# Hybrid four-branch layer on one core: the recurrent branch woven at weight 48 instead of 26, the last tiles' modulation split between two engines, and the next branch's operand loaded three chunks earlier in the merge

## The chip, the cores and the metric

The kernel runs on one core of a Trainium2 chip. The metric is device microseconds of one execution. The five engines run their own instruction queues in order: PE (TensorE, matrix products), ACT (ScalarE), DVE (VectorE), POOL (GpSimd) and SP (SyncE, which here only issues DMAs). ACT issues DMAs too.

## The reference

Two layers (DEPTH = 2) work on 1024 latent tokens and 256 context tokens of width 1024. One input projection feeds four mixers and their gates; the mixers' outputs are merged and projected:

```python
p_lat = (layer_norm(x) * (1.0 + scale) + shift) @ w_in
...
ya = merge_heads(neighbourhood_attention(q, k, v, kc, vc, na_rel_bias))     # branch A
yb = merge_heads(prefix_attention(q, k, v, kc, vc, MLA_SCALE))              # branch B
yc, yc_c = rglru_mixer(lat[6], cx[6], ...)                                  # branch C, recurrent
yd = merge_heads(prefix_attention(q, k, v, kc, vc, GQA_SCALE))              # branch D
...
acc = sum(jax.nn.sigmoid(ms[i]) * ((ys[i] * jax.nn.silu(zs[i])) @ w_branch[i]) for i in range(N_BRANCH))
x_new = layer_norm(DEEPNORM_ALPHA * x + gate * (acc @ w_out)) * ln_g + ln_b
```

The recurrent branch computes, for each direction, `r` and `i` by sigmoids of small products, `a = exp(log_a)`, `u = sqrt(1 - a*a) * i * x`, and a linear scan along the tokens.

## The kernel before

All ten 128-token tiles (two of context, eight latent) stay in SBUF as pairs `xh`, `xl`: a value in float32 is split into a rounded high part and a low rest, and a product is three matmuls (high by high, high by low, low by high: L299 to L301 and L307 to L309). The split is done by `hi_lo` (ACT copies the high part at L312, DVE subtracts at L313) or, for weights, by `split_w` (L263, L264).

A layer runs in these stages, and the names of tiles in the profile begin with the stage that made them.

- `g_proj`, the projection of branch D.
- A stage in which two generators are woven. The main one chains `m_proj` (branch B, 12 steps), one step that loads the first attention operands, and `a_proj` (branch A: ten 512-column tiles for q and k, then ten 256-column tiles for v; some 20 steps). The other is `lru_steps` (branch C), for each of two halves of 128 channels: a projection, a convolution, then for each direction the products with sigmoids (L515), tanh (L522), exp (L523), sqrt (L528), and the scans; then `put_u`, which multiplies the branch's output with its gate. That is 24 steps a half in layer 0 and 20 in layer 1. `weave` always advances the stream with the least `(steps done + 0.5) / weight`: the main one has weight `W_A = 30`, the other `W_B = 26`. A weight is only a rate; a stream that is left goes on alone.
- Attention for the three branches (`g_att`, `m_att`, `a_att`), with the products of half of the merge gates ("gates", `g_att__mm` and so on) as filler for PE. Before it, `cut_memory` gives the same SBUF out anew; a new tile waits until the old ones at its place have been read.
- `merge`: for each branch in the order 2, 3, 1, 0 and each of 8 chunks of 128 columns, the gate's product (even chunks) or its stored value from DRAM (odd chunks), its sigmoid, the branch product, and the sum. At the head of each branch `load_u` brings the branch's output in from DRAM and splits it. All of this goes through the rotating pool `tmp` of 3 buffers, and all loads through SP's queue. In layer 0 the next layers' modulation vectors (`mod`) are computed beside it.
- `outp`: output projection, residual, two norms. In layer 0 `xm_tile` then makes the next layer's `xh`, `xl` for a tile: for each half of 4 blocks, four PE transposes into a PSUM bank (`tbank`), four ACT operations that scale and shift (L243; a DVE form stands in L245 but `V_ACT = 4` never takes it), and a split. `tbank` has two banks, and a third one (the bank of attention's `pv`) while `wide_t[0]` is set, which it isn't in `outp`.

The engines' final order is made by a scheduler that keeps dependences and follows program order as a priority, so instructions of neighbouring steps mix.

Of the kernel before, what the change touches and what calls it, by code (L numbers as in the profile page):

```python
# [17 lines left out]
KC = D // 128  # L18
# [3 lines left out]
TT = NT // 128  # L22
# [7 lines left out]
V_ACT = 4  # L30
# [4 lines left out]
X_ACT = (0, 2)  # L35
M_ORDER = (2, 3, 1, 0)
W_A = 30
W_B = 26
Z_0, GATE_0 = 2, 10
UNITS = [(2, 3), (5, 3), (8, 2)]  # L40
AHEAD = 2
# [6 lines left out]
def hybrid_kernel(ctx: ExitStack, tc, a):  # L48
# [27 lines left out]
    def nm(s):  # L76
        ids[0] += 1
        return f"{phase[0]}__{s}_{ids[0]}"
# [4 lines left out]
    def weave(*streams):  # L83

        live = [[0, n, label, gen] for label, gen, n in streams]
        while live:
            s = min(live, key=lambda s: (s[0] + 0.5) / s[1])
            phase[0] = s[2]
            s[0] += 1
            if next(s[3], live) is live:  # L90
                live.remove(s)
# [11 lines left out]
    def chain(*parts):  # L103
        for label, gen in parts:
            while True:
                phase[0] = label
                if next(gen, parts) is parts:
                    break
                yield

    def mm():
        return ps_mm.tile([128, 512], F32, tag="mm", name=nm("mm"))

    turns = [0, 0, 0]
    wide_t = [False]

    def sbank():

        turns[1] = (turns[1] + 1) % 3
        return wide[:, 512 * turns[1]:512 * turns[1] + 512]  # L120

    def tbank():
        turns[2] = (turns[2] + 1) % 3
        if wide_t[0] and not turns[2]:
            return ps_v.tile([128, 512], F32, tag="pv", name=nm("t"))
        return ps_t.tile([128, 512], F32, tag="t", name=nm("t"))
# [13 lines left out]
    def kept(which, dt=F32, w=NT, s="kept"):  # L140

        return kv.tile([128, w], dt, tag=which, name=nm(s))

    def slot(dt=F32, w=NT, s="sl"):
        return cut["sl"].tile([128, w], dt, tag="sl", name=nm(s))

    def tmp(w=512, dt=F32):
        return tp.tile([128, w], dt, tag="tmp", name=nm("tmp"), bufs=3)
# [81 lines left out]
    def xm_tile(t, xn, mc, xh, xl):  # L230
        s = 1 if t < CT else 0
        ts = slice(t * 128, (t + 1) * 128)
        for h in range(2):
            pt = tbank()
            v = tmp()
            for i in range(4):
                k = 4 * h + i
                pe.transpose(pt[:, i * 128:(i + 1) * 128], xn[:, k * 128:(k + 1) * 128], ident)
            for i in range(4):
                k = 4 * h + i  # L240
                o, src = v[:, i * 128:(i + 1) * 128], pt[:, i * 128:(i + 1) * 128]
                if i < V_ACT:
                    act.activation(o, src, AF.Identity, bias=mc[:, s, k:k + 1], scale=mc[:, s, 8 + k:9 + k])  # L243
                else:
                    dve.tensor_scalar(o, src, mc[:, s, 8 + k:9 + k], mc[:, s, k:k + 1], ALU.mult, ALU.add)  # L245
            v3 = v.rearrange("p (k t) -> p k t", k=4)
            hi_lo(xh[:, 4 * h:4 * h + 4, ts], xl[:, 4 * h:4 * h + 4, ts], v3)
# [22 lines left out]
    def load_w(src, shape, far=False, by_pool=False):  # L270
        n = 1
        for d in shape[1:]:
            n *= d
        raw = cut["wp"].tile([128, 512], F32, tag="wraw", name=nm("wraw"), bufs=2)
        dst = raw[:, :n]
        if len(shape) == 3:
            dst = dst.rearrange("p (a b) -> p a b", a=shape[1])
        sp.dma_start(dst, src)
        return split_w(raw, shape, far, by_pool)
# [4 lines left out]
    def load_chunk(w3, by_pool=False):  # L284

        out = []
        nk = w3.shape[1]
        for k0 in range(0, nk, 4):
            kk = min(4, nk - k0)
            hi, lo = load_w(w3[:, k0:k0 + kk, :], [128, kk, 128], by_pool=by_pool)  # L290
            out += [(hi[:, i, :], lo[:, i, :]) for i in range(kk)]
        return out
# [10 lines left out]
    def mm_b(ps, ws, xs, first=True, last=True):  # L303
        nk = len(ws)
        for k in range(nk):
            (wh, wl), (xh, xl) = ws[k], xs(k)
            pe.matmul(ps, wh, xh, start=first and k == 0, stop=False)  # L307
            pe.matmul(ps, wh, xl, start=False, stop=False)  # L308
            pe.matmul(ps, wl, xh, start=False, stop=last and k == nk - 1)  # L309

    def hi_lo(hi, lo, src):
        act.copy(hi, src)  # L312
        dve.tensor_sub(lo, src, hi)  # L313

    def layer(l, xh, xl, need_ctx, gate, finish, side, ahead=None):
# [11 lines left out]
        def xs_g(g):  # L327
            gs = slice(g[0], g[0] + g[1])
            return lambda k: (xh[:, k, gs], xl[:, k, gs])
# [471 lines left out]
        def a_steps():  # L801
            wa = load_rows(w_in, C_A, 512)
            prev = None
            for t, ps in project(wa, lambda t: 0 if t >= q0t else 256, 512):
                c0 = 0 if t >= q0t else 256
                y = tmp()
                if c0 == 0:
                    act.activation(y[:, :256], ps[:, :256], AF.Copy, scale=0.125)
                act.copy(y[:, 256:], ps[:, 256:])  # L809
                if prev:  # L810
                    put_t(*prev)
                prev = qk_a, t, c0 // 128, [y[:, c:c + 128] for c in range(c0, 512, 128)]
                yield
            put_t(*prev)
            wv = load_rows(w_in, C_AV, 256)
            for t, ps in project(wv, lambda t: 0, 256):
                put_v(v_a, t, ps[:, :256].rearrange("p (h e) -> p h e", e=64))
                yield
# [126 lines left out]
        def first_loads():  # L945
            next(att)
            yield


        weave(("", chain((f"m_proj{l}", m_steps()), (f"g_att{l}", first_loads()), (f"a_proj{l}", a_steps())), W_A),  # L950
              (f"lru{l}", lru_steps(), W_B))
        wide_t[0] = False
# [10 lines left out]
        def load_u(i, keep):  # L963
            uh, ul = [], []
            for c in range(2):
                if keep and c == 0:
                    th, tl = kept("k", F32R, s="uh"), kept("v", F32R, s="ul")
                else:
                    th, tl = slot(F32R, s="uh"), slot(F32R, s="ul")
                for g in qgroups:  # L970
                    gs = slice(g[0], g[0] + g[1])
                    t = tmp(g[1])
                    sp.dma_start(t, u_d[i][c, :, gs])
                    hi_lo(th[:, gs], tl[:, gs], t)
                uh.append(th)
                ul.append(tl)
            return uh, ul

        def merge():
            for bi, i in enumerate(M_ORDER):  # L980
                uh, ul = load_u(i, bi % 2 == 0)
                for c in range(KC):
                    w = None if (i, c) in gate_d else load_chunk(a["w_chunks"][l, GATE_0 + i * KC + c])
                    wb = load_chunk(a["w_branch"][l, i, c])
                    if bi == 0:
                        acc[c] = slot(s="acc")
                    for g in qgroups:
                        gs = slice(g[0], g[0] + g[1])
                        sgm = tmp()
                        if w is None:  # L990
                            pm = sgm
                            sp.dma_start(sgm[:, :g[1]], gate_d[i, c][:, gs])
                        else:
                            pm = mm()
                            mm_b(pm[:, :g[1]], w, xs_g(g))
                        act.activation(sgm[:, :g[1]], pm[:, :g[1]], AF.Sigmoid)
                        pb = sbank()
                        mm_b(pb[:, :g[1]], wb, lambda k: (uh[k][:, gs], ul[k][:, gs]))
                        if bi == 0:
                            dve.tensor_mul(acc[c][:, gs], pb[:, :g[1]], sgm[:, :g[1]])  # L1000
                        else:
                            dve.tensor_mul(sgm[:, :g[1]], pb[:, :g[1]], sgm[:, :g[1]])  # L1002
                            (pool if w is None else dve).tensor_add(acc[c][:, gs], acc[c][:, gs], sgm[:, :g[1]])  # L1003
                        yield
# [29 lines left out]
        chunks = list(range(x0, NT, 256))  # L1034


        phase[0] = f"outp{l}"
        gain = [[cut["wp"].tile([128, 512], F32, tag=tag, name=nm(src)) for _ in range(2)]
                for tag, src in (("whi", "ln_g"), ("wlo", "ln_b"))]
# [126 lines left out]
    def fin0(t, Y, later):  # L1166
        if t >= CT:
            sp.dma_start(x1[(t - CT) * 128:(t - CT + 1) * 128, :], Y)
        layer_norm(Y, LN2_ACT)
        later.append(partial(xm_tile, t, Y, mc1["m"], xh, xl))  # L1170
# [96 lines left out]
```

## Time and profile before

| | |
|---|---|
| time, median of 3 runs | 2960.34 us (2957.03 to 2962.0) |
| time of the profiled execution | 2960.92 us |
| its span, first to last instruction | 2959.1 us |
| PE, DVE, ACT, POOL busy | 94%, 51%, 41%, 14% of the span |
| TensorE clock granted, mean | 0.977 of full speed |
| HBM traffic | 101 GB/s over the span |

The profile gives, for one execution, when each instruction ran on its engine, what ended each idle time, and the granted TensorE clock (1.0 is the upper of its two levels, 2.4 GHz; 0.5 the lower, 1.2 GHz). PE is the busiest engine, so idle PE and PE at the lower clock are what can be won.

### The profile page before, as it was taken

The page shows a single profiled execution, that of the slowest core. Times are in us where ns is not written, and L with a number is a line of the kernel's source. Part 1 is how long each engine was busy: PE and PEld are TensorE (multiplying, and loading weights), DVE is VectorE, ACT ScalarE, POOL GpSimd, SP SyncE. Part 2 cuts the span into 40 slices and gives each one's busy share as a digit, 9 for nine tenths or more (in the row PEclk, how much of TensorE's full clock was granted, in tenths as well). Part 3 has the DMA queues.
Part 4 walks back from the last instruction along what each step waited for, and adds up shares of the span by engine and source line. Part 5 has one row for each costly group of instructions (what it writes and reads, how often), then busy time and mean ns, then how long its engine had stood idle before and what let it go on. Part 6 is the DMA issues. An engine that isn't in the chain of part 4 may idle for free.

```text
span 2959.1 us, 40218 instructions
## 1 busy us (share of the span) xinstructions
PE 2790.4 (94%) x14458; PEld 2253.0 (76%) x14458; DVE 1508.0 (51%) x3069; ACT 1219.0 (41%) x2631; POOL 418.8 (14%) x507
## 2 busy tenths in 40 slices
PE   7997979999999999899999798999999999999998
PEld 3785858888888887677767576778888888777776
DVE  5644266555555552232458554356555556533456
ACT  4344256445455542222234434346545455522230
POOL 1210020110111100111222120012111111001131
PEclk9998989999999999999999898999999999999999
DMA  6333322222223333333332333423222323222232
GB/s 248 115 107 102 107 72 84 84 84 87 88 88 123 103 98 111 104 120 104 124 98 90 91 103 111 117 74 102 80 93 78 106 103 126 87 94 87 86 109 91
DMA packets 240424, 301.83 MB, mean 102 GB/s; under 512 B 27488, under 2 KB 160096, under 8 KB 240224
## 3 DMA queue, kind: packets, MB, share of 16 engines
q1 hardware_dynamic: 134368, 225.58, 24.2%
q10 hardware_dynamic: 105856, 73.68, 8.0%
q8 instruction: 114, 1.87, 0.3%
q14 instruction: 86, 0.70, 0.1%
HBM read 217.11 MB, written 82.07 MB: 101 GB/s over the span
## 4 chain that ended last, share of the span: by engine, by line
PE 75%; DVE 7%; DMA 4%; ACT 4%; issue 2%; POOL 2%; ACTq 1%; SPq 0%; DVEq 0%; POOLq 0%
PE wide L639 6%; PE merge__mm L307 4%; PE merge__mm L308 4%; PE merge__mm L309 4%; PE wide L307 3%; PE wide L308 3%; PE wide L309 3%; PE m_att__t L584 3%; PE g_att__t L584 2%; PE a_att__mm L307 2%; PE a_att__mm L308 2%; PE a_att__mm L309 2%; PE m_att__mm L309 2%; PE m_att__mm L308 2%; PE m_att__mm L307 2%
## 5 line engine op out<-in xcount | busy, mean ns | idle before, releaser
L307 PE MATMUL merge__mm<-xh,merge__whi 128*128 128x512 f32 (+1 forms) x640 | 243.0, 380 | 0.9 <-ACT a_att__tmp L934 0.9
L308 PE MATMUL merge__mm<-xl,merge__whi 128*128 128x512 f32 (+1 forms) x640 | 239.6, 374 | 0.0
L309 PE MATMUL merge__mm<-xh,merge__wlo 128*128 128x512 f32 (+1 forms) x640 | 239.4, 374 | 0.0
L313 DVE TENSOR_TENSOR m_att__pl<-m_att__t,m_att__ph 128x384 fp32r<-128x384 f32 (+1 forms) x248 | 122.1, 508 | 117.2 <-ACT m_att__ph L312 78.8
L263 ACT CAST merge__whi<-merge__wraw 128x256 fp32r<-128x256 f32 (+1 forms) x128 | 65.6, 513 | 255.6 <-PE merge__mm L308 176.7
L1002 DVE TENSOR_TENSOR merge__tmp<-wide,merge__tmp 128x512 f32<-128x512 f32 (+1 forms) x120 | 76.5, 637 | 184.8 <-PE wide L309 161.2
L1003 POOL TENSOR_TENSOR merge__acc<-merge__acc,merge__tmp 128x512 f32<-128x512 f32 (+1 forms) x60 | 79.2, 1320 | 585.9 <-DVE merge__tmp L1002 585.8
L307 PEld LDWEIGHTS merge__mm<-xh,merge__whi 128*128 128x128 f32 x640 | 120.6, 188 | 44.5 <-issue 19.9
L312 ACT CAST m_att__ph<-m_att__t 128x384 fp32r<-128x384 f32 (+1 forms) x248 | 105.0, 439 | 115.3 <-PE m_att__t L584 103.5
L313 DVE TENSOR_TENSOR g_att__pl<-g_att__t,g_att__ph 128x384 fp32r<-128x384 f32 (+1 forms) x228 | 111.3, 514 | 79.6 <-ACT g_att__ph L312 58.4
L307 PE MATMUL wide<-merge__uh,merge__whi 128*128 128x256 f32 (+1 forms) x320 | 127.4, 398 | 20.4 <-ACT merge__uh L312 11.5
L264 DVE TENSOR_TENSOR merge__wlo<-merge__wraw,merge__whi 128x256 fp32r<-128x256 f32 (+1 forms) x128 | 71.0, 555 | 141.2 <-ACT merge__whi L263 134.3
L309 PEld LDWEIGHTS merge__mm<-xh,merge__wlo 128*128 128x128 f32 x640 | 120.8, 189 | 23.9 <-issue 0.4
L308 PEld LDWEIGHTS merge__mm<-xl,merge__whi 128*128 128x128 f32 x640 | 120.8, 189 | 22.3
L312 ACT CAST g_att__ph<-g_att__t 128x384 fp32r<-128x384 f32 (+1 forms) x228 | 97.7, 446 | 69.3 <-PE g_att__t L584 65.3
L307 PE MATMUL a_att__mm<-xh,a_att__whi 128*128 128x512 f32 (+1 forms) x320 | 123.8, 387 | 0.0
L641 DVE TENSOR_SCALAR_CACHE_REDUCE m_att__p<-wide 128x1280 f32<-128x1280 f32 (+1 forms) x72 | 98.7, 1371 | 42.1 <-PE wide L639 41.8
L309 PE MATMUL a_att__mm<-xh,a_att__wlo 128*128 128x512 f32 (+1 forms) x320 | 120.1, 377 | 0.0
L639 PE MATMUL wide<-g_att__ks,g_att__q 128*128 128x512 f32 (+1 forms) x400 | 103.5, 365 | 17.5 <-DVE g_att__p L641 16.3
L308 PE MATMUL a_att__mm<-xl,a_att__whi 128*128 128x512 f32 (+1 forms) x320 | 120.0, 375 | 0.0
L299 PE MATMUL a_proj__mm<-a_proj__whi,xh 128*128 128x256 f32 (+1 forms) x320 | 112.0, 351 | 8.1 <-ACT a_proj__tmp L809 4.5
L308 PE MATMUL wide<-merge__ul,merge__whi 128*128 128x256 f32 (+1 forms) x320 | 119.6, 374 | 0.0
(418 smaller groups left out, 7919.4 us busy)
## 6 DMA issues: line engine op xcount, KB each, us to landing
merge__wraw<-in_w_chunks_dram SPq DMA_DIRECT2D x64, 256.0 KB, 2.9
mod__wm<-in_w_mod_dram SPq DMA_DIRECT2D x64, 256.0 KB, 3.0
g_proj__wm<-in_w_mod_dram SPq DMA_DIRECT2D x16, 512.0 KB, 9.8
a_att__wraw<-in_w_chunks_dram SPq DMA_DIRECT2D x32, 256.0 KB, 2.7
merge__wraw<-in_w_branch_dram SPq DMA_DIRECT2D x64, 128.0 KB, 2.1
merge__tmp<-start__gates SPq DMA_DIRECT2D x32, 256.0 KB, 3.2
merge__tmp<-outp__gates SPq DMA_DIRECT2D x32, 256.0 KB, 3.4
g_att__wraw<-in_w_chunks_dram SPq DMA_DIRECT2D x28, 256.0 KB, 2.7
```

The lines of the kernel that those rows point to most:

```text
L264: (pool if by_pool else dve).tensor_sub(lo[:, :n], raw[:, :n], hi[:, :n])
L299: pe.matmul(ps, xh, wh[:, n0:n1], start=first and k == 0, stop=False)
L307: pe.matmul(ps, wh, xh, start=first and k == 0, stop=False)
L308: pe.matmul(ps, wh, xl, start=False, stop=False)
L309: pe.matmul(ps, wl, xh, start=False, stop=last and k == nk - 1)
L312: act.copy(hi, src)
L313: dve.tensor_sub(lo, src, hi)
L584: pe.transpose(tb[:, i * 128:(i + 1) * 128], pts[q0 + i][:, col:col + 128], ident)
L639: pe.matmul(wide[:, c0:c0 + w], qs[:, j, qi * 128:(qi + 1) * 128], k[:, c0:c0 + w], start=j == 0, stop=j == len(ks) - 1)
L641: dve.tensor_scalar(pt[:, :nk], wide[:, :nk], -scale, None, ALU.mult, ALU.min, accum_out=nb)
L1002: dve.tensor_mul(sgm[:, :g[1]], pb[:, :g[1]], sgm[:, :g[1]])
L1003: (pool if w is None else dve).tensor_add(acc[c][:, gs], acc[c][:, gs], sgm[:, :g[1]])
```

## The change

Four edits. `W_B` becomes 48, so `lru_steps` advances faster against the main stream. In `xm_tile` the last four tiles take the ACT form for two blocks of each half and the DVE form for the other two. In `merge` each next branch's `load_u` stands before chunk 5 of the branch at hand instead of behind its last chunk. And `wide_t[0]` is set before `outp`, so `tbank` hands out three banks there.

```diff
-W_B = 26
+W_B = 48
...
-                if i < V_ACT:
+                if i < (V_ACT if t < TT - 4 else 2):
                     act.activation(o, src, AF.Identity, bias=mc[:, s, k:k + 1], scale=mc[:, s, 8 + k:9 + k])
                 else:
                     dve.tensor_scalar(o, src, mc[:, s, 8 + k:9 + k], mc[:, s, k:k + 1], ALU.mult, ALU.add)
...
         def merge():
+            ready = load_u(M_ORDER[0], True)
             for bi, i in enumerate(M_ORDER):
-                uh, ul = load_u(i, bi % 2 == 0)
+                uh, ul = ready
                 for c in range(KC):
+                    if c == KC - 3 and bi < 3:
+                        ready = load_u(M_ORDER[bi + 1], bi % 2 == 1)
...
         chunks = list(range(x0, NT, 256))
...
+        wide_t[0] = True
         phase[0] = f"outp{l}"
```

First place: ACT's queue in layer 0 where the second channel half of branch C computes its sigmoids (L515), exponentials (L523) and roots (L528). Before, from the last rows of `a_proj`'s v tiles on (L312 casts `vt`, L362 stores it; L459 is the tanh of `put_u`):

```order
L312 CAST a_proj__vt_3285<-a_proj__mm_3220 128x4x64
L312 CAST lru__lruh_3281<-lru__lruc_3273 128x1280
L362 DMA start__va_106<-a_proj__vt_3269 128x4x128
L362 DMA start__va_106<-a_proj__vt_3285 128x4x128
L515 ACT_TABLE_LOAD
L515 ACTIVATE lru__lrug_3299<-wide,lrucols 128x256
L459 ACTIVATE lru__tmp_3411<-lru__mm_3386 128x256
L515 ACTIVATE lru__lrug_3299<-wide,lrucols 128x512 x2
```

And now, where L808 and L809 bring a q and k tile of `a_proj` out of PSUM:

```order
L515 ACTIVATE lru__lrug_2807<-wide,lrucols 128x256
L522 ACTIVATE lru__lrut_2859<-lru__lrug_2755,lrusp_312 128x1280
L515 ACTIVATE lru__lrug_2807<-wide,lrucols 128x512
L523 ACT_TABLE_LOAD
L523 ACTIVATE lru__lrug_2755<-lru__lrug_2755,lrusp_311 128x1280
L515 ACT_TABLE_LOAD
L515 ACTIVATE lru__lrug_2807<-wide,lrucols 128x512
L808 ACTIVATE a_proj__tmp_2845<-a_proj__mm_2820 128x256
L809 COPY a_proj__tmp_2845<-a_proj__mm_2820 128x256
L312 CAST a_proj__th_2853<-a_proj__t_2848 128x512
```

The group stood behind all of `a_proj`'s products and now stands among its q and k tiles; between the first sigmoid and the last root of this half there are now four such tiles.

Second place: SP's queue in layer 0 at the end of the merge's first branch (`start__u` is the next branch's output, `start__gates` a stored gate, `wm` the modulation's weights, `last__gate` the gate vector written out element by element). Before:

```order
L973 DMA merge__tmp_11680<-start__u_26_128 128x256
L973 DMA merge__tmp_11684<-start__u_26_128 128x512
L180 DMA mod__bm_13147<-in_b_mod_dram 128x8
L1014 DMA last__gate_13919<-mod__modc_11666 128x8x1 x2
L278 DMA merge__wraw_12015<-in_w_branch_dram 128x256
L973 DMA merge__tmp_11688<-start__u_26_128 128x512
```

And now:

```order
L973 DMA merge__tmp_11454<-start__u_26_128 128x512
L185 DMA mod__wm_11570<-in_w_mod_dram 128x512
L973 DMA merge__tmp_11460<-start__u_26_128 128x256
L185 DMA mod__wm_11608<-in_w_mod_dram 128x512
L973 DMA merge__tmp_11464<-start__u_26_128 128x512
L185 DMA mod__wm_11663<-in_w_mod_dram 128x512
L973 DMA merge__tmp_11468<-start__u_26_128 128x512
L995 DMA merge__tmp_11479<-start__gates_9_111 128x256
```

The six loads of the next branch now stand in front of chunk 5's gates (`gates_9`) and before the element-wise gate vector; before, they stood around that vector, some 25 rows later.

Third place: DVE's queue at the end of `outp` in layer 0 (L216 and L225 belong to the last tile's norm, L313 writes `xl`). Before:

```order
L214 BN_STATS outp__bnst_15047<-outp__Y_14871 128x6 x2
L313 TENSOR_TENSOR xl<-outp__tmp_15059,xh 128x4x128
L216 BN_AGGR outp__mv_15050<-outp__bnst_15047 128x2
L225 SCALAR_TENSOR_TENSOR outp__nb_15055<-outp__mv_15050,outp__rs_15052 128x1
L313 TENSOR_TENSOR xl<-outp__tmp_15071,xh 128x4x128
L313 TENSOR_TENSOR xl<-outp__tmp_15083,xh 128x4x128
```

And now:

```order
L214 BN_STATS outp__bnst_15047<-outp__Y_14871 128x6 x2
L245 TENSOR_SCALAR outp__tmp_15059<-outp__t_15058,mod__modc_13160 128x128
L216 BN_AGGR outp__mv_15050<-outp__bnst_15047 128x2
L245 TENSOR_SCALAR outp__tmp_15059<-outp__t_15058,mod__modc_13160 128x128
L225 SCALAR_TENSOR_TENSOR outp__nb_15055<-outp__mv_15050,outp__rs_15052 128x1
L245 TENSOR_SCALAR outp__tmp_15071<-outp__t_15070,mod__modc_13160 128x128 x2
```

Of the sixteen new DVE operations two stand before the last norm's `nb` and fourteen behind it; ACT has sixteen fewer.

## Rows read from the trace of the kernel before

**Rows 1.** The page: busy us (share of the span) and instructions of each engine.
```profile
PE 2790.4 (94%) x14458; PEld 2253.0 (76%) x14458; DVE 1508.0 (51%) x3069; ACT 1219.0 (41%) x2631; POOL 418.8 (14%) x507
```

**Rows 2.** Windows: start:end, length, busy us (count) by engine, PE clock, DMA share.
```profile
193.00:270.00 77.00, 57.91 (x250) 45.39 (x249) 35.45 (x77) 42.00 (x88) 5.93 (x12) 0.84 0.41 119
...
370.00:430.00 60.00, 41.44 (x206) 33.09 (x205) 35.85 (x34) 31.78 (x39) 18.11 (x12) 0.86 0.23 73
...
1800.00:1870.00 70.00, 51.12 (x217) 40.28 (x216) 31.54 (x62) 35.69 (x71) 4.68 (x9) 0.80 0.37 107
...
1930.00:2010.00 80.00, 72.88 (x390) 60.80 (x391) 41.38 (x41) 38.12 (x49) 19.56 (x16) 0.98 0.26 78
...
1188.00:1212.00 24.00, 16.35 (x65) 11.53 (x64) 6.97 (x14) 5.09 (x10) 0.00 (x0) 0.86 0.51 90
...
1625.00:1650.00 25.00, 10.50 (x46) 7.20 (x46) 15.88 (x30) 22.87 (x54) 3.16 (x6) 0.62 0.17 63
```

**Rows 3.** PE's waits, 370 to 432 us: total, times, longest.
```profile
PE wide L639 <- DVE g_att__p L641: 14.9, 3, 14.0
```

**Rows 4.** DVE in order of time around attention's start in layer 0.
```profile
424.47 0.42 DVE L641 TENSOR_SCALAR_CACHE_REDUCE g_att__p<-wide 128x256 f32<-128x256 f32 x1 [3.13 <-DMA start__u<-lru__lruo]
```

**Rows 5.** ACT's groups, 193 to 270 us: count, busy, mean ns, idle before.
```profile
L515 ACT ACTIVATE lru__lrug<-wide,lrucols 128x512 f32<-128x512 f32 x8 | 5.5, 688 | 5.2 <-PE wide L309 5.2
...
L523 ACT ACTIVATE lru__lrug<-lru__lrug,lrusp 128x1280 f32<-128x1280 f32 x2 | 2.7, 1362 | 0.0
...
L515 ACT ACTIVATE lru__lrug<-wide,lrucols 128x256 f32<-128x256 f32 x4 | 1.9, 473 | 5.8 <-DMA start__qkm<-m_proj__th 3.4 <-PE m_proj__t L348 2.4
...
L808 ACT ACTIVATE a_proj__tmp<-a_proj__mm 128x256 f32<-128x256 f32 x2 | 0.8, 384 | 0.0
```

**Rows 6.** ACT in order of time: a DMA issue, and a table load between two operations.
```profile
191.85 0.54 ACTq L355 DMA_DIRECT2D start__qkm<-m_proj__th  x1
...
223.19 1.28 ACT L515 ACT_TABLE_LOAD   x1
224.48 0.69 ACT L515 ACTIVATE lru__lrug<-wide,lrucols 128x512 f32<-128x512 f32 x1
```

**Rows 7.** PE's waits, 195 to 300 us.
```profile
PE a_proj__t L348 <- ACT a_proj__tmp L808: 2.8, 3, 2.3
PE a_proj__mm L299 <- ACT a_proj__tmp L809: 2.2, 1, 2.2
```

**Rows 8.** The chain, 270 to 300 us: start, us, what.
```profile
299.59 0.23 PE a_proj__mm L301
```

**Rows 9.** PE's waits, 1930 to 2040 us (layer 1).
```profile
PE wide L639 <- DVE g_att__p L641: 1.4, 3, 1.0
```

**Rows 10.** PE in order of time at the merge's first change of branch.
```profile
1203.49 0.58 PE L307 MATMUL wide<-merge__uh,merge__whi 128*128 128x256 f32 x1 [7.65 <-ACT merge__uh L312]
```

**Rows 11.** DMA issues, 1185 to 1205 us: count, KB, us to landing.
```profile
merge__tmp<-start__u SPq DMA_DIRECT2D x4, 256.0 KB, 6.8
...
last__gate<-mod__modc SPq DMA_DIRECT2D x2, 4.0 KB, 11.1
```

**Rows 12.** PE's waits in layer 1's merge, 2560 to 2840 us.
```profile
PE wide L307 <- ACT merge__uh L312: 2.7, 3, 1.2
```

**Rows 13.** ACT and DVE in order of time at the end of outp, layer 0.
```profile
1640.89 0.62 ACT L312 CAST xh<-outp__tmp 128x512 fp32r<-128x512 f32 x1
1641.40 1.51 ACT L243 ACTIVATE outp__tmp<-outp__t,mod__modc 128x128 f32<-128x128 f32 x4
...
1645.36 0.69 DVE L313 TENSOR_TENSOR xl<-outp__tmp,xh 128x512 fp32r<-128x512 f32 x1 [1.22 <-ACT xh L312]
```

**Rows 14.** SP's waits, 1600 to 1680 us.
```profile
SPq L278 <- PE outp__t L238: 8.3, 1, 8.3
```

**Rows 15.** DVE's groups in xm_group, whole span: count, busy, mean ns.
```profile
L1132 DVE TENSOR_SCALAR g_proj__v<-g_proj__t,g_proj__modc 128x512 f32<-128x512 f32 x8 | 6.4, 804 | 0.0
...
L1132 DVE TENSOR_SCALAR g_proj__v<-g_proj__t,g_proj__modc 128x256 f32<-128x256 f32 x4 | 2.1, 542 | 0.1
```

## The prediction

> **What bounds the kernel now.** I read the page first: PE is busy 2790 of 2959 us [rows 1], and over the long attention and merge stages hardly idle. So the change can only win where PE stands still or runs at the lower clock. I then cut the span into stretches of 100 and of 10 us and kept those where PE's busy time falls short. In each row of [rows 2] the reader should take two numbers: the length less PE's busy time (idle), and that busy time multiplied by one less the granted clock (about what the lower clock costs).
>
> From 193 to 270 us (layer 0, end of `m_proj` beside the first half of branch C) that is 19.1 idle and 57.9 x 0.16 = 9.3 to the clock, 28 together. From 370 to 430 (layer 0, second half of C, start of attention) it is 18.6 and 5.8, together 24. Layer 1's two stretches of the same work, 1800 to 1870 and 1930 to 2010, have 18.9 and 10.2, together 29, and 7.1 and 1.5, together 9. Layer 0's first change of branch in the merge, 1188 to 1212, has 7.7 and 2.3, together 10. The end of `outp` in layer 0, 1625 to 1650, has 14.5 and 4.0, together 18.
>
> Then I asked PE's waits in each stretch for the reason. In 370 to 430 it is one wait of 14.0 us: the first scores wait for DVE to read a score bank into a `g_att__p` tile [rows 3], and DVE had to wait 3.13 us more for branch C's output to be stored [rows 4]: the new tile lies where the old output lay. So the tail of branch C, running alone, holds attention up. In layer 1 the same hand-over costs 1.4 us [rows 9], since the filler and the v tiles cover it. In 193 to 270 the waits are spread over ACT's work, `a_proj`'s evacuations with 2.8 and 2.2 us among them [rows 7]. At the change of branch it is one wait of 7.65 us for `uh` [rows 10]; loads of `start__u` took 6.8 us there, beside a 4 KB write of the gate vector that took 11.1 us [rows 11].
>
> **Edit 1, the weight.** Main steps are 33, C's are 48 and 40. At 26 to 30, C has about 29 steps done when the main stream ends: 19 are left alone in layer 0, 11 in layer 1. At 48, C is through after 30 and 25 main steps. No instruction is added but two table loads; the work moves.
>
> *The tail in layer 0.* The 24 us of 370 to 430 go, except a hand-over as in layer 1, 1.4 us [rows 9], called 2. But the second half's sigmoids, exponentials and roots now sit among `a_proj`'s q and k tiles, and what that costs no row shows directly. I price ACT's queue there. A half has 8 table loads at 1.28 [rows 6], 10.2 us; 8 sigmoids of 512 columns at 0.688 and 4 of 256 at 0.473, 7.4; six operations of 1280 columns (tanh, exp, sqrt, twice), all at exp's 1.362, 8.2 [rows 5]; four tiles with two copies at 0.384 [rows 5] and one cast at 0.62 [rows 13], 5.6; six DMA issues at 0.54 [rows 6], 3.2. Sum 34.6 us. PE has there four tiles of 24 matmuls at 0.23 [rows 8], 22, and C's gate products, 36 matmuls at 0.23 or, for 256 columns, half of it, 7; with the next tile begun, 29 to 35. So ACT is longer by 0 to 6 us, before any waiting of one for the other. Bounds from stretches: below, 9, which the half costs in layer 1 now beside v tiles; above, 28, which the first half costs beside `m_proj`, whose steps go between PE and ACT many more times [rows 2]. I take 12, nearer to the lower one, since a q and k tile passes ACT twice only and has two banks. Layer 0: 24 - 2 - 12 = 10 gained (6 lost to 13 gained by the bounds).
>
> *Layer 1.* The 9 us of 1930 to 2010 become the same 12: 3 lost (19 lost to 0).
>
> *The first half.* It stays among `m_proj` steps in both layers, but moves ahead of the end of that stage, so `a_proj`'s first evacuations no longer stand behind exponentials: 2.8 + 2.2 us in layer 0 [rows 7]. `m_proj`'s own evacuations take part of that place. I count 2 a layer, 4 in all (8 lost to 12 gained, half of that stretch's idle time either way being about as far as a reshuffle of the same work goes).
>
> Edit 1 in all: 10 - 3 + 4 = 11 us.
>
> The Trainium skill, "ScalarE: Activation LUTs", section "What ACT_TABLE_LOAD costs", gives 1283 ns for the load and about 1380 ns of drain for every switch, some 2.66 us. Here the operation behind a load starts 1.29 us after the load does [rows 6], so the trace shows the first part and no drain behind it; the sum above goes by the row. By the page the half would cost ACT 21 us in loads in place of 10, and the 12 would become 23.
>
> **Edit 3, the loads ahead.** At layer 0's first change of branch the six loads now stand ahead of the gate vector's write, so both the 7.65 us wait and the lower clock behind it go: 10 us. The other changes of branch were nearly free: in layer 1 all waits for `uh` are 2.7 us [rows 12], part of it the first branch's, which doesn't move; I count 1. Against this stands a new wait. The six tiles (four in layer 1) pass a pool of three buffers, and chunk 5's stored gates stand behind them in SP's queue and pool, as do modulation loads between them that wait for PE. PE can run on over chunk 5's products (18 matmuls, six of them of 256 columns, 3.5 us) and two of chunk 6's gate products (24 matmuls of 256 columns and 24 of 512, 8.3 us): 12 us. Two rounds of three loads at 6.8 us [rows 11] would be 14. So a wait of about 0 to 3 at each of six places; I take 4 in all. Edit 3: 10 + 1 - 4 = 7 us (0 to 12).
>
> **Edits 2 and 4, the last tiles.** In 1625 to 1650 ACT is busy 22.9 of 25 us [rows 2]. A half tile costs it 1.51 for four blocks and 0.62 for the cast [rows 13]; now 0.76 + 0.62 = 1.4. DVE gets two operations of 128 columns out of PSUM, which no row shows. From 804 ns at 512 columns and 542 at 256 [rows 15] a line gives 411 at 128; so DVE has 0.82 + 0.69 = 1.5 a half. Fourteen of the sixteen stand behind the last norm, with seven subtractions: 14 x 0.41 + 7 x 0.69 = 10.6 us on DVE, where ACT has about five halves of 2.1 now. So the bound moves to DVE and little is won; the third bank lets the last transposes go earlier, and the next layer's first weights wait for those, 8.3 us [rows 14]. I take 2 (0 to 6, sixteen ACT operations at 0.38). Layer 1's `outp` makes no such tiles.
>
> **Sum.** 11 + 7 + 2 = 20 us off the profiled execution's 2960.9: 2941; the median of the runs stands 0.6 lower, so **2940 us**.
>
> **The rivals.**
>
> *ACT becomes the bound in `a_proj` (slower).* For it: the 28 us that the first half costs beside `m_proj`, with ACT's operations in strict order before PE's banks come free. Against: PE stayed nearly full in 1930 to 2010 with the same half beside v tiles. If the half costs 28 in both layers, layer 0 loses 6, layer 1 19; with 4 + 7 + 2 from the rest that is 12 slower, 2972. It is slower than before from 22 us a half on, where 22 - 22, 9 - 22 and the 13 of the rest cancel. Chance 0.11.
>
> *Table switches hold ACT longer than their rows.* The eight loads of a half would cost their 10.2 us once more in idle time behind them, the half 22, and the sum comes to nothing: 2960. The Trainium skill's section on what a load costs, named above, would have it so. Against it the 1.29 us from load to next operation [rows 6]. Chance 0.03.
>
> *PE covers it all.* The half costs 5 beside q and k tiles (the 0 to 6 by which ACT's queue is longer), and the first half wins 10 of its 57: 17 + 4 + 10, with 10 and 2 from the other edits, 43 faster, 2917 (the halves of C with 5, the merge without its new waits). For it: ACT is busy only 42 of 77 us from 193 to 270 [rows 2]. Against: that stretch lost 19 all the same. Chance 0.18.
>
> *The hand-over stays.* If the first `p` tiles lie where weights or v stores of `a_proj` are still in use, attention's start waits for these instead, and the 24 us shrink by no more than the second half's new cost: 0 - 3 + 4 + 7 + 2, 10 faster, 2950. For it: `a_proj` ends later than before, and the memory is cut anew all the same. Against: layer 1 hands over in 1.4 us with weights just read. Chance 0.14. That nothing is reordered is excluded by the queues.
>
> **How the numbers follow.** The forecast itself has 0.54, with a range of its own from 2928 to 2955. A difference of 0.2%, 6 us, is about what a measurement of this kernel can tell from none. Faster are all of the forecast's but 0.03, all of the case in which PE covers it, and 0.11 of that in which the hand-over stays: 0.80. Slower is the case with ACT as the bound but for 0.01: 0.10. The rest, with the table switches, is the same: 0.10. The range from 2914 to 2960 takes in all but the slower rival (0.11) and the lower part of PE covering it all (0.08).
>
> **What would show it.** Right: a wait of `g_att` scores on DVE of under 4 us in place of 14.0; PE idle 4 to 9 us more in the q and k part of `a_proj` in both layers; no wait for `uh` over 3 us at the first change of branch; waits at chunks 5 and 6 of some us; the last `outp` transposes 1 to 3 us closer to the stretch's start. Wrong: idle time of over 15 us where the second half's exponentials now stand, or a first half that costs other than 20 to 30 us.

## The result: 1.1% faster, and the profile after

| | before | after |
|---|---|---|
| median, same chip | 2958.69 us (2955.18 to 2962.0) | 2924.69 us (2923.69 to 2926.0) |
| ratio | | 0.9886, 95% interval 0.9868 to 0.9903 |
| profiled execution, span | 2960.92, 2959.1 us | 2926.0, 2924.2 us |
| PE busy; mean clock | 2790.4 us; 0.977 | 2782.2 us; 0.979 |

The time lies in the range, but below the 2928 to 2955 that the forecast had for itself: 34 us were won where 20 were forecast. From the first instruction of each stage in the two traces (of the merge, from its first branch product): layer 0, from `m_proj` to the first scores of branch B, 506.9 us before and 499.5 after (7.4 won); layer 0's merge 402.0 and 388.5 (13.5 won), its output stage 154.7 and 156.3 (1.6 lost); layer 1's `g_proj` 69.6 and 68.1 (1.5 won); layer 1, `m_proj` to the same point, 454.7 and 441.7 (13.0 won); the rest within 0.8 a stage. From `m_proj` to branch B's scores, the layer in which the prediction had edit 1 lose won more than the other.

The stretches of the kernel after, with the columns of [rows 2]:

```profile
180.00:240.00 60.00, 43.16 (x183) 34.94 (x182) 35.79 (x71) 35.80 (x72) 12.72 (x17) 0.77 0.21 59
310.00:360.00 50.00, 50.00 (x247) 40.50 (x246) 26.76 (x27) 34.81 (x49) 0.00 (x0) 1.00 0.25 72
270.00:280.00 10.00, 5.05 (x12) 3.32 (x13) 3.50 (x6) 4.28 (x9) 0.00 (x0) 0.57 0.62 182
360.00:375.00 15.00, 8.20 (x43) 6.90 (x42) 8.84 (x14) 4.59 (x9) 0.00 (x0) 0.77 0.47 131
1770.00:1850.00 80.00, 61.91 (x291) 50.75 (x290) 39.52 (x88) 36.30 (x84) 9.01 (x14) 0.87 0.45 131
1860.00:1920.00 60.00, 58.03 (x265) 45.56 (x264) 30.01 (x30) 35.31 (x52) 0.00 (x0) 1.00 0.27 77
```

```profile
167.60:222.80 55.20, 40.88 (x189) 33.13 (x187) 25.79 (x52) 34.04 (x68) 10.22 (x16) 0.82 0.22 61
1736.60:1789.90 53.30, 44.65 (x205) 35.93 (x203) 25.94 (x57) 33.50 (x66) 10.22 (x16) 0.91 0.22 62
1789.90:1850.00 60.10, 48.12 (x235) 41.22 (x236) 32.23 (x77) 22.50 (x61) 5.94 (x10) 0.88 0.53 157
```

Read each as before, length less PE busy, then PE busy by one less the clock. Branch C's second halves stand in 310 to 360 (layer 0) and 1860 to 1920 (layer 1): PE loses 0 and 2.0 us, at the upper clock, while ACT has its 35 us of work. The stretches at the end of `m_proj`, 180 to 240 and 1770 to 1850, still lose 16.8 + 9.9 = 27 and 18.1 + 8.0 = 26. That is not the price of the first halves alone. From its first sigmoid to its last root the first half runs from 167.6 to 222.8 in layer 0 and from 1736.6 to 1789.9 in layer 1, and there PE loses 14.3 + 7.4 = 22 and 8.7 + 4.0 = 13. In layer 1 another 12.0 + 5.8 = 18 go behind it, in 1789.9 to 1850, where none of its sigmoids, exponentials or roots is left. And two stretches of layer 0, 270 to 280 and 360 to 375, lose 5.0 + 2.2 and 6.8 + 1.9, together 16, where [rows 2] has none.

PE's waits in the kernel after, 240 to 300 us and then 300 to 430 us (total, times, longest):

```profile
PE a_proj__mm L299 <- ACT a_proj__whi L263: 6.2, 1, 6.2
```

```profile
PE a_proj__mm L299 <- ACT a_proj__whi L263: 3.7, 3, 2.2
PE a_proj__mm L300 <- DVE a_proj__wlo L264: 3.0, 1, 3.0
...
PE wide L639 <- DVE g_att__p L641: 0.5, 1, 0.5
```

The 14.0 us wait of [rows 3] has become 0.5. What stands in its place is the weights of `a_proj`: first those of q and k, then those of v, are late.

SP's waits in the kernel after, 350 to 358 us, and then its loads in order of time, 300 to 378 us (start, length of the issues, what):

```profile
SPq L651 <- PE wide L309: 29.2, 1, 29.2
SPq L278 <- DVE a_proj__wlo L264: 4.3, 1, 4.3
```

```profile
310.51 3.13 SPq L278 DMA_DIRECT2D a_proj__wraw<-in_w_in_dram  x2
350.31 2.50 SPq L651 DMA_DIRECT2D g_att__q<-start__qkg  x4
356.87 13.55 SPq L278 DMA_DIRECT2D a_proj__wraw<-in_w_in_dram  x6
```

Two v weights are loaded at 310. Then SP stands 29.2 us before `g_att`'s first query tile (L651): the trace names as its releaser branch C's gate products (L309), which read the tiles in whose place it is to lie. The other six v weights are behind it in the queue and start at 356.9. But the queue is not what they wait for last. Raw weights pass two buffers (`wraw`, `bufs=2`), and both are full from some 316 us on, since these loads take 2.0 us to land. They come free when ACT has cast and DVE has subtracted:

```profile
353.37 0.69 ACT L515 ACTIVATE lru__lrug<-wide,lrucols 128x512 f32<-128x512 f32 x1
353.96 0.40 ACT L263 CAST a_proj__whi<-a_proj__wraw 128x256 fp32r<-128x256 f32 x1
```

```profile
355.02 1.48 DVE L521 TENSOR_TENSOR lru__lrug<-lru__lrug,lru__lruc 128x1280 f32<-128x1280 f32 x1
356.42 0.75 DVE L264 TENSOR_TENSOR a_proj__wlo<-a_proj__wraw,a_proj__whi 128x256 fp32r<-128x256 f32 x2
```

ACT takes the first weight up some 40 us after it has come, in its order right behind the second half's last sigmoid (and the second 1.1 us later); DVE follows behind one of the half's products; and SP, past its query tile, stands 4.3 us more for the buffer.

In layer 0's merge the changed kernel's DMA issues (count, KB, us to landing) and PE's waits are:

```profile
merge__tmp<-start__u SPq DMA_DIRECT2D x14, 256.0 KB, 3.6
...
last__gate<-mod__modc SPq DMA_DIRECT2D x2, 4.0 KB, 10.7
```

```profile
PE wide L307 <- DVE merge__tmp L1005: 2.5, 4, 0.8
...
PE wide L307 <- ACT merge__uh L312: 0.8, 1, 0.8
```

A load of `start__u` lands in 3.6 us (the median), the 7.65 us wait of [rows 10] is gone, and no wait at chunks 5 and 6 has come for it. The 6.8 us of [rows 11] are the median of two kinds of loads. In the kernel before, of those issued from 1187.9 to 1189 us, ahead of the gate vector's write, and of those from 1191.5 to 1194, behind it:

```profile
merge__tmp<-start__u SPq DMA_DIRECT2D x1, 256.0 KB, 3.4
```

```profile
merge__tmp<-start__u SPq DMA_DIRECT2D x2, 256.0 KB, 10.4
```

In the kernel after, the write takes as long, and what is issued behind it (1182 to 1192 us) is as late, but no `start__u` is among it:

```profile
mod__wm<-in_w_mod_dram SPq DMA_DIRECT2D x1, 256.0 KB, 9.1
merge__wraw<-in_w_branch_dram SPq DMA_DIRECT2D x1, 128.0 KB, 8.7
```

The end of `outp` in layer 0, PE's waits in 1600 to 1635 us, and DVE in order of time:

```profile
PE outp__t L238 <- DVE outp__tmp L245: 8.1, 3, 6.5
...
PE outp__t L238 <- ACT outp__tmp L243: 2.0, 2, 1.3
```

```profile
1613.06 1.41 DVE L1077 SCALAR_TENSOR_TENSOR outp__Y<-outp__Y,outp__mv,outp__ln_g 128x512 f32<-128x512 f32 x2
...
1616.85 1.28 DVE L214 BATCH_NORM_STATS2 outp__bnst<-outp__Y 128x6 f32<-128x512 f32 x2
1618.04 0.40 DVE L245 TENSOR_SCALAR outp__tmp<-outp__t,mod__modc 128x128 f32<-128x128 f32 x1
```

The transposes have waits of 10.9 us in all, 8.1 of them on DVE. The first split operation stands in DVE's order behind the last tile's statistics (L214); the bank waits for it until 1618.

### The profile page after: what moved, and what is told of

Its sections match the earlier page's. It is cut to its first block, busy times and chain, and to the rows that moved or that the text cites. A ratio compares the mean times of both kernels' runs of the same rounds, so it can differ in the third digit from the quotient of the medians.

```text
span 2924.2 us, 40179 instructions
## 1 busy us (share of the span) xinstructions
PE 2782.2 (95%) x14458; PEld 2248.4 (77%) x14458; DVE 1503.1 (51%) x3085; ACT 1219.3 (42%) x2617; POOL 420.1 (14%) x507
## 5 line engine op out<-in xcount | busy, mean ns | idle before, releaser
L309 PE MATMUL merge__mm<-xh,merge__wlo 128*128 128x512 f32 (+1 forms) x640 | 238.5, 373 | 0.0
L313 DVE TENSOR_TENSOR m_att__pl<-m_att__t,m_att__ph 128x384 fp32r<-128x384 f32 (+1 forms) x248 | 122.0, 508 | 117.5 <-ACT m_att__ph L312 78.8
L263 ACT CAST merge__whi<-merge__wraw 128x256 fp32r<-128x256 f32 (+1 forms) x128 | 65.8, 514 | 249.3 <-PE merge__mm L308 172.9
L313 DVE TENSOR_TENSOR g_att__pl<-g_att__t,g_att__ph 128x384 fp32r<-128x384 f32 (+1 forms) x228 | 112.8, 515 | 88.3 <-ACT g_att__ph L312 56.0
L312 ACT CAST m_att__ph<-m_att__t 128x384 fp32r<-128x384 f32 (+1 forms) x248 | 105.2, 440 | 115.0 <-PE m_att__t L584 105.3
L309 PEld LDWEIGHTS merge__mm<-xh,merge__wlo 128*128 128x128 f32 x640 | 120.3, 188 | 23.8 <-issue 0.4
L312 ACT CAST g_att__ph<-g_att__t 128x384 fp32r<-128x384 f32 (+1 forms) x228 | 98.2, 446 | 83.3 <-PE g_att__t L584 78.7
L641 DVE TENSOR_SCALAR_CACHE_REDUCE g_att__p<-wide 128x1280 f32<-128x1280 f32 (+1 forms) x72 | 98.6, 1369 | 45.9 <-PE wide L639 35.7
L309 PE MATMUL a_att__mm<-xh,a_att__wlo 128*128 128x512 f32 (+1 forms) x320 | 120.0, 377 | 0.0
L299 PE MATMUL a_proj__mm<-a_proj__whi,xh 128*128 128x256 f32 (+1 forms) x320 | 110.3, 346 | 9.9 <-ACT a_proj__whi L263 9.8
```

What stands on the lines that cost most here:

```text
L299: pe.matmul(ps, xh, wh[:, n0:n1], start=first and k == 0, stop=False)
L641: dve.tensor_scalar(pt[:, :nk], wide[:, :nk], -scale, None, ALU.mult, ALU.min, accum_out=nb)
```

## The experiments

The two theories told apart here are the record's terms (edit 1 worth 11 us, edit 3 worth 7, edits 2 and 4 worth 2) and the reading of the trace after (20, 14, 0). Ratios are against the kernel before in the same chip's runs.

**Edit 1 alone**, on the kernel before.

```diff
-W_B = 26
+W_B = 48
```

> The kernel before with W_B = 48 alone. The record's sum makes edit 1 worth 11 us (10 in layer 0's tail, 3 lost in layer 1, 4 from the first halves): a ratio of 0.9963. The trace of the changed kernel reads otherwise, 7 us less in layer 0's projections and 13 less in layer 1's, so 20 us: a ratio of 0.993. Under 0.9945 the trace's reading holds and layer 1 gained where the record has it lose; over 0.996 the record's sum holds and the layer-1 gain came from another edit.

Measured 2936.57 us against 2960.31: ratio 0.9923 (0.9911 to 0.9935), 24 us by the medians. The trace's reading holds. By stages, layer 0 from `m_proj` to the merge won 8.4 us (972.1 to 963.7), layer 1 from `m_proj` to branch B's scores 12.8 (454.7 to 441.9). The second halves, with the columns of [rows 2]:

```profile
310.00:360.00 50.00, 49.72 (x246) 40.21 (x244) 27.07 (x28) 34.80 (x49) 0.00 (x0) 1.00 0.26 74
1870.00:1930.00 60.00, 59.14 (x270) 46.63 (x269) 29.66 (x30) 35.37 (x53) 0.00 (x0) 1.00 0.26 76
```

They cost 0.3 and 0.9 us, not 12, and edit 1 alone brings the late weights too: its wait on L263 in 250 to 300 us is 6.1.

**Edit 3 alone**, on the kernel before (`load_u` of the next branch ahead of chunk 5, as in the diff).

> The kernel before with the merge's loads ahead alone. The record: 11 us won at the changes of branch, 4 lost to new waits at chunks 5 and 6, so 7 us, ratio 0.9976. By the trace of the changed kernel layer 0's merge is 13.5 us shorter, with no new waits at chunks 5 and 6, and layer 1's 0.8: 14 us, ratio 0.9952. If the merge's gain came in part from edit 1 (another state of the loads at the merge's start), this run shows less than 10.

Measured 2947.5 us: 0.9963 (0.9949 to 0.9976), 13 us by the medians and 11 by the ratio. Layer 0's merge went from 402.0 to 389.5 us, the output stage behind it from 154.7 to 157.2. That is nearer to the trace's reading. The interval, 7.1 to 15.1 us, leaves the record's 7 at its edge.

**Edits 2 and 4 alone**, on the kernel before.

> The kernel before with the last tiles' split and the third bank alone. The record: 2 us won (0 to 6), the bound moving to DVE. The trace of the changed kernel: layer 0's output stage 1.6 us longer and the next projection 1.5 shorter, so 0; a time 0 to 2 us above the kernel before would make these two edits idle or harmful.

Measured 2960.87 us: 1.0004 (0.9995 to 1.0014). They are worth nothing. The wait on L245 is here too, 7.6 us, the longest 6.0. The three ratios add to 0.0110 off, the changed kernel has 0.0114: within the noise the edits neither help nor hinder one another.

**The changed kernel without edit 2.**

```diff
-                if i < (V_ACT if t < TT - 4 else 2):
+                if i < V_ACT:
```

> The changed kernel with edit 2 taken back (four ACT operations a half again), edit 4 kept. The record makes the split worth 2 us, so this is 2 us slower than the changed kernel, some 2927. If the 6.5 us wait of a transpose on DVE, seen at the end of the output stage, is a loss that the split brought, this is 2 to 6 us faster, 2919 to 2923. If ACT and DVE cost the same there, it is equal within 1.

Measured 2924.51 us, 0.9883 (0.9868 to 0.9898): equal. The 6.5 us wait on DVE is no loss that could be had back; with four ACT operations the transposes wait 9.8 us on ACT in its place.

**The kernel before without the gate vector's write.** Only `last__gate` and its reading back are left out.

```diff
-        for s in range(2):
-            sp.dma_start(gd[s].rearrange("(k p) -> p k", p=128), gate["m"][:, s, :KC])
...
-                        bcast(gt[s], gd[s], 1024)
+                        bcast(gt[s], a["ln_g"][l], 1024)
```

> The kernel before without the element-by-element write of the gate vector at the end of the modulation; the last product is multiplied by ln_g in place of the gate, so the output is another. If that write held up the loads of the next branch (11.1 us for 4 KB, beside 6.8 for 256 KB), the 7.65 us wait for uh at the first change of branch falls under 3 and the time by 5 to 10 us, as edit 3 alone gave. If the loads were only issued too late, the wait stays over 5 us and the time within 3 of the kernel before.

Measured 2951.94 us: 0.9973 (0.9963 to 0.9984), 8 us. PE's waits at the same place, 1090 to 1300 us, and the loads' time to landing, 1180 to 1200 us, in that kernel:

```profile
PE wide L307 <- DVE merge__tmp L1002: 4.0, 4, 2.1
PE wide L307 <- ACT merge__uh L312: 0.4, 1, 0.4
```

```profile
merge__tmp<-start__u SPq DMA_DIRECT2D x4, 256.0 KB, 3.5
```

So the loads were in time as they stood; the write of 2 x 4 KB in 4-byte pieces held up those behind it. Edit 3 wins by passing that write, and taking the write away wins about as much (4.7 to 11.0 us by the interval, edit 3 alone 7.1 to 15.1).

**Are the weights of `a_proj` late for want of buffers?** Three versions of the changed kernel: v weights packed two to a buffer; this with 11 pairs and 10 slots; and this with the first two packed weights loaded behind the sixth q and k tile.

```diff
-            wv = load_rows(w_in, C_AV, 256)
+            wv = []
+            for k in range(0, KC, 2):
+                hi, lo = load_w(w_in[k * 128:(k + 2) * 128, C_AV:C_AV + 256].rearrange("(a p) n -> p a n", p=128),
+                                [128, 2, 256])
+                wv += [(hi[:, i, :], lo[:, i, :]) for i in range(2)]
...
-        cut_memory(f"a{l}", 11, 10)
+        cut_memory(f"a{l}", 10, 11)
...
+                if t == 5:
+                    load_v_pair(0)
+                    load_v_pair(2)
```

> The changed kernel with the eight v weight tiles of a_proj (256 columns each) packed two to a buffer, so that they need four pairs in place of eight and half as many loads and splits. Theory: in layer 0 edit 1 took away the cover under which these weights came, and PE now stands 4.9 us and runs 1.7 us longer for it around 360 to 370 us; packed, that stretch closes and the time falls by 4 to 7 us, to about 2919, with no wait for the v weights over 1 us. Rival: the weights are not what is late, but the stores or reads behind them; then the wait changes its name and the time stays within 2 us of 2925.

> The same with one more weight pair and one slot less (10 and 11 in place of 11 and 10). Theory of too few pairs: the wait for the q and k weights of layer 0, 6.1 us at about 272 us, becomes shorter by one load and split, 1 to 2 us. Rival: slots are as short as pairs, and branch C's tiles then wait for one another: slower by 2 us or more.

> The version with packed v weights and 11 pairs, with the first two of the four packed v weights loaded and split behind the sixth q and k tile instead of behind the last. Theory: the v weights come late because ACT splits them behind all its work on the q and k tiles, and two raw buffers let no more be loaded before; with half of them split early the 5 us wait at 360 us goes, and the time is 3 to 6 us under the 2920 of that version. If pairs are what is short, the early split waits itself, and the time is the same or longer.

Measured 2924.19 (0.9878, 0.9864 to 0.9891), 2919.82 (0.9862, 0.9849 to 0.9876) and 2921.31 us (0.9860, 0.9841 to 0.9880). The theory missed: the waits for v weights were 6.7 us in the changed kernel, and 5.7, 5.0 and 5.0 here. In the second, the wait for the q and k weights is 6.8, not shorter; what it gained is not located. The early loads didn't help either: three of the four packed weights were loaded and two of them split by 315 us, and the fourth, again behind L651's 29.2 us wait in SP's queue, was issued at 355.9. That might look like SP's queue, where the load of attention's first operands waits for branch C. But the third weight had come 47 us before ACT cast it, and ACT cast the fourth right behind it:

```profile
312.07 0.38 SPq L278 DMA_DIRECT2D a_proj__wraw<-in_w_in_dram  x1
```

```profile
361.44 1.14 ACT L263 CAST a_proj__whi<-a_proj__wraw 128x512 fp32r<-128x512 f32 x2 [2.46 <-issue]
```

DVE subtracts these two from 364.5 on, behind branch C's last scan (L537) and sum (L541). So the trace names the order of ACT and DVE. This version moved only the first half of the casts ahead; no version moved the others, so the cause is read from traces and not shown by a run of its own.

**Where branch C stands.** Three more places in the changed kernel: `W_B = 40` (through some three steps behind the main stream in layer 0), `W_B = 96` (both halves beside `m_proj` and the first tiles of `a_proj`), and held back by `HOLD = 30` empty steps, at `W_B = 72`, until `m_proj` is through:

```diff
+        def held():
+            for _ in range(HOLD):
+                yield
+            yield from lru_steps()
...
-              (f"lru{l}", lru_steps(), W_B))
+              (f"lru{l}", held(), W_B))
```

> The changed kernel with W_B = 40: branch C is through after 36 main steps' worth in layer 0, some 3 steps behind the end of the main stream, and after 30 in layer 1. If a tail alone is what costs (24 us for 19 steps left alone), 3 to 4 steps cost some 4 us, while branch C's products cover the late v weights' 6.6: 2 to 3 us faster than the changed kernel. If the second half cost ACT's time among the q and k tiles as the record has it (12 us), moving it out of them would win more, 5 us or over.

> The changed kernel with W_B = 96: branch C is through before m_proj is, so both halves' sigmoids, exponentials and roots stand beside m_proj's steps. Theory: what stands beside a half decides its price; ACT has the same 35 us for it in either place, and PE loses about 26 us beside m_proj's short dependent steps and under 1 beside the 24-matmul tiles of a_proj. Then the second halves cost some 20 to 26 us more in each layer, less the late weights that this covers: 2955 to 2975. Rival: the price is ACT's load alone, which beside m_proj is no greater; then this stays within 10 us of the changed kernel's 2925.

> The changed kernel with branch C held back for 30 empty steps and W_B = 72, so that it begins when m_proj's steps are through and both halves stand beside a_proj. Theory of the neighbour: the first halves lose their 26 us a layer, and m_proj alone loses part of that for want of other work: 2880 to 2905. Rival, the record's: two halves give ACT 70 us of work beside a_proj's own, PE waits for ACT there, and what the first half saves is paid again: 2920 to 2950.

Measured 2923.2 (0.9872, 0.9859 to 0.9886), 2915.86 (0.9844, 0.9828 to 0.9860) and 2919.4 us (0.9866, 0.9846 to 0.9885). At 40 the time is equal to the changed kernel's within the noise; whether the 5 us or over that the record's 12 would give back have come is not decided by it. The theory that a half costs 26 us wherever it stands beside `m_proj` fell outright: forecast 2955 to 2975, measured 2915.9. The theory of the neighbour fell too: 2880 to 2905 for the held version, which came out just under its rival's 2920 to 2950. The stretches of `W_B = 96` with its first half, its second half, and what follows it:

```profile
150.00:215.00 65.00, 54.59 (x263) 45.75 (x263) 34.86 (x68) 38.92 (x75) 8.16 (x18) 0.92 0.20 54
255.00:310.00 55.00, 46.84 (x215) 36.17 (x214) 31.59 (x52) 36.65 (x62) 4.71 (x8) 0.94 0.23 65
310.00:330.00 20.00, 11.19 (x49) 8.35 (x48) 11.53 (x19) 6.65 (x15) 0.00 (x0) 0.74 0.63 190
```

Worked out as above, 14.8 and 11.0 us for the stretches of the halves, and 11.7 behind them. Beside the same neighbours the first half alone, from its first sigmoid to its last root, loses 6.7 + 1.3 = 8 here and 22 in the changed kernel:

```profile
151.70:191.90 40.20, 33.53 (x167) 28.06 (x166) 19.52 (x33) 28.33 (x47) 4.67 (x9) 0.96 0.10 28
```

One difference is in PE's waits: the up-projections of `m_proj` (`wide` L299) wait 6.7 us for C's sigmoids to empty a bank in the changed kernel, 1.7 here. The held version gave up the first half's waits beside `m_proj` and got others (5.0 us for an operation of `put_u` on DVE, 4.2 for attention's first gate weights). All three lie 37 to 46 us under the kernel before, 11 to 13 of them from edit 3: what they share with the changed kernel is that C no longer stands at the end alone, or hardly.

**The two best together**: `W_B = 96`, packed v weights, 11 pairs and 10 slots.

> W_B = 96 together with the packed v weights, 11 pairs and 10 slots. W_B = 96 alone ran in 2915.9 and packing with 11 pairs in 2919.8, 8.8 and 4.9 under the changed kernel's 2924.7. If the two gains lie in different waits they add: about 2911. If both only take away the cover that the late weights lacked, they do not: 2915 to 2920.

Measured 2909.49 us: 0.9831 (0.9816 to 0.9846). That is near the 2911 of two gains that add, but the interval of `W_B = 96` alone, 0.9828 to 0.9860, overlaps, so the sum is not shown. In both versions PE has no wait for `a_proj`'s weights left in layer 0 (120 to 430 us), and SP's wait before L651 is short too, 2.4 us here and 3.0 with `W_B = 96` alone, since C's tiles are free by then. So these two runs don't part SP's queue from the order of ACT and DVE; the late casts above do.

## Why the prediction was right in sign and short in size

**The tail in layer 0**, 24 - 2 - 12 = 10: the sum was nearly met, by luck. The tail's 24 us went and the hand-over costs 0.5. The sign set for the 12, idle time of 4 to 9 us among the q and k tiles, was not there: 0 and 2.0. The failed term is "what that costs no row shows directly ... I take 12". ACT's work came out near its price (34.6 us forecast, 34.81 busy in 310 to 360, though with six tiles in it and without the DMA issues), but it was set against PE work of 29 to 35 us for four tiles. With the step on DVE and the scans between them, the sigmoids and roots spread over 50 us, six q and k tiles and C's own products; ACT is 70% busy and PE has no gap. The lower bound of 9 was no bound: it put all of PE's idle time in 1930 to 2010 down to the half. From the half's first sigmoid to its last root PE lost 3.7 in the kernel before:

```profile
1955.90:1988.20 32.30, 28.57 (x157) 23.72 (x157) 16.11 (x15) 26.27 (x31) 0.61 (x1) 1.00 0.24 70
```

In place of the 12 came 16 us for late weights, which the prediction didn't see. The kernel before has 0.3 us of such waits from 200 to 400 us; 23 of C's matmuls of 512 columns stand there between 314 and 334, where the v weights are changed. In the kernel after they are gone from that place, and ACT and DVE come to the v weights only behind the second half. So the prediction's mechanism, the half ahead of `a_proj`'s work in ACT's order, does cost something, but at the weights and not at the tiles; and the moved work had been a cover at its old place. How much of the 16 is either stays open.

**Layer 1**, 3 lost: wrong in sign, by the same term. 9 became 2.0 us, 7 won; the stretch of the first half went from 29 to 26. A further part comes from a place that the prediction doesn't name. The 24 matmuls of 256 columns of C's input projection now stand in `g_proj`, where there were none before, in a wait of PE's for DVE at the stage's end. The first product of `m_proj` in the kernel before, and C's first one and that of `m_proj` in the kernel after:

```profile
1718.66 0.31 PE L299 MATMUL m_proj__mm<-m_proj__whi,xh 128*128 128x160 f32 x1 [3.90 <-DVE g_proj__tmp L423]
```

```profile
1694.10 0.36 PE L307 MATMUL wide<-xh,lru__whi 128*128 128x256 f32 x1
...
1698.06 0.31 PE L299 MATMUL m_proj__mm<-m_proj__whi,xh 128*128 128x160 f32 x1 [0.89 <-DVE g_proj__tmp L423]
```

So the stage behind is spared some 3 us of work, and `g_proj` is 1.5 us shorter with them in it. With those, 7 + 3 + 3 + 1.5 = 14.5, what was measured over both stages.

**The first half**, 2 a layer: near it by the stretches (28 to 27 and 29 to 26), which take in more than the half. The two waits that it named, 2.8 and 2.2 us, are down to 0.5, but others came. By the half's own bounds PE lost 29 in either layer before, and 22 and 13 after, so the sign "other than 20 to 30" did show in layer 1, with most of the gain given back behind the half:

```profile
194.40:273.40 79.00, 59.91 (x252) 46.75 (x251) 37.27 (x78) 43.23 (x89) 5.93 (x12) 0.83 0.41 117
1787.30:1870.50 83.20, 64.32 (x286) 51.99 (x285) 36.98 (x79) 43.14 (x90) 5.75 (x12) 0.84 0.39 112
```

**Edit 3**, 10 + 1 - 4: the first term holds (1190 to 1210 us lost 9.9 in slices of 10, the slices there now 0 and 0.7). The waits at chunks 5 and 6 were mis-sized at 4 and are 0: they were priced with the 6.8 us of [rows 11], a median between loads held up by the gate write and loads that were not. Undisturbed loads take 3.6, two rounds 7, and PE's cover of 12 is enough.

**Edits 2 and 4**, 2 (0 to 6): at the lower bound. DVE's part behind the last norm was sized well (10.6 forecast; from 1619.7 to 1629.8 in the trace), and one operation takes 0.40 us as estimated at 0.41. But the two that stand ahead of the last norm's end hold a bank for 6.5 us in DVE's strict order, and without edit 2 the transposes wait on ACT instead. The third bank's lead gained nothing with either form.

**The rivals.** Nearest came the one in which PE covers it all (2917, chance 0.18): its half costs 5 where 0 to 2 were measured, its merge has no new waits, but its first half wins 10, where the stretches won 1 to 3. The hand-over did not stay, ACT did not become the bound, and the table switches, with eight loads a half, stand in stretches in which PE loses 0 and 2.0 us. The Trainium skill, "ScalarE: Activation LUTs", section "What ACT_TABLE_LOAD costs", would have had some 1380 ns of drain with each; the trace doesn't agree, since in the kernel after too a load starts at the end of the operation ahead of it, and the operation behind it starts 1.29 us after the load (below: start, us, what).

```profile
332.69 1.36 ACT L523 ACTIVATE lru__lrug<-lru__lrug,lrusp 128x1280 f32<-128x1280 f32 x1
334.07 1.28 ACT L515 ACT_TABLE_LOAD   x1
335.36 0.69 ACT L515 ACTIVATE lru__lrug<-wide,lrucols 128x512 f32<-128x512 f32 x1
```

## What to carry to other kernels

When work is moved, price both ends: what it meets at its new place, and what it was covering at the old one (here both bear on the change of weights, 16 us in layer 0). A cost that no row shows should be set against the neighbour's whole stretch and not against a few rows of the order; 35 us of ACT work beside 50 us of long matmul chains cost those chains nothing. A load that stands behind a blocked one need not be late for that: see whether it had a buffer to land in, and who was to empty it. And a median taken beside a disturbance, as the 6.8 us here, can be the price of no load at all.

## What the runs showed that was not expected

Writing 2 x 4 KB as single elements took 10.7 to 11.3 us in three traces (before, after, edit 3 alone) and made the loads issued right behind it land in some 9 to 10 us in place of 3.5, a cost of 8 us to the whole kernel (4.7 to 11.0). And where branch C stands, at weights from 40 to 96 or held back, moved the time by only 9 us, 2915.9 to 2924.7, although from its first sigmoid to its last root PE loses 22 us in layer 0 of the changed kernel, 13 in layer 1 and 8 in layer 0 with `W_B = 96`; what sets that price beyond the shared bank stays open.
